# Instance norm over 4 MB units: statistics for pairs of units, and one normalise per engine

## The chip, the cores and the metric

The kernel runs on one core of a Trainium2 chip. The metric is device time in microseconds (us) of one launch, the median of several launches. All data is fp32 and lies in HBM before and after. Launches of one kernel agree within some 0.3%; a difference under 2% counts as "same".

## The reference

```python
# x: (4, 8, 16, 256, 256) fp32, gamma: (8, 16) fp32
mu  = x.mean(axis=(3, 4), keepdims=True)
var = ((x - mu) ** 2).mean(axis=(3, 4), keepdims=True)
out = (x - mu) / np.sqrt(var + 1e-5) * gamma[None, :, :, None, None]
```

There are 512 channels of 65,536 values, 134.22 MB in and 134.22 MB out. Each channel needs its mean and variance before its first value can be written.

## The kernel before

The kernel takes 16 channels at a time, a "unit" of 4 MB: a tile of 128 partitions by 8192 columns, 8 partitions to a channel. There are 32 units and 6 tiles. SyncE issues the loads, ScalarE's sequencer issues the stores. A load into a tile waits until the store out of it has landed. VectorE sums a unit, ScalarE squares it and accumulates, a small matmul adds over the 8 partitions of a channel, and both engines share the normalise.

```python
data = ctx.enter_context(tc.tile_pool(name="data", bufs=6))
...
def load(u):
    t = data.tile([P, F], F32, name="xt")          # P = 128, F = 8192
    for a, b in load_spans.get(u, whole):          # one span: the whole unit
        nc.sync.dma_start(out=t[:, a:b], in_=xv[u, :, a:b])
    tiles[u] = t
for u in range(6):
    load(u)
...
def coefficients(u):
    ...
        nc.vector.reduce_sum(out=sums[:, j : j + 1], in_=t[:, a:b], axis=AX.X)
        for c in range(a, b, SQ):                  # SQ = 4096: two squares
            nc.scalar.activation(
                out=junk[:], in_=t[:, c : c + SQ], func=ACTF.Square,
                accum_out=sqs[:, n : n + 1],
            )
    ... # add the parts up, matmul, copy out of PSUM, negate, variance
    std = stats_pool.tile([P, 1], F32, name="std")
    nc.scalar.activation(out=std[:], in_=var[:], func=ACTF.Sqrt, bias=eps_t[:], scale=1.0)
    ... # reciprocal, scale, shift
for u in range(U):
    scale, shift = coefficients(u)
    t = tiles.pop(u)
    ...
        norm_vector(t, 0, DV, scale, shift)        # DV = 5376 columns
        norm_scalar(t, DV, F, scale, shift)
        nc.scalar.dma_start(out=ov[u], in_=t[:])
    if u + 6 < U:
        load(u + 6)
```

Of the kernel before, what the change touches and what calls it, by code (L numbers as in the profile page):

```python
# [6 lines left out]

F32 = mybir.dt.float32
BF16 = mybir.dt.bfloat16
ALU = mybir.AluOpType  # L10
ACTF = mybir.ActivationFunctionType
AX = mybir.AxisListType


@with_exitstack
def kernel(
    ctx: ExitStack,
    tc: tile.TileContext,
    x: bass.AP,
    gamma: bass.AP,  # L20
    out: bass.AP,
):
    nc = tc.nc
    B, G, C, H, W = x.shape
    P = nc.NUM_PARTITIONS
    HW = H * W
    n_ch = B * G * C
    S = 8
    K = P // S
    F = HW // S  # L30
    U = n_ch // K
    NG = (G * C) // K
    SQ = 4096
    DV = 5376
    assert HW % S == 0 and (G * C) % K == 0 and F % SQ == 0

    xv = x.rearrange("b g c h w -> (b g c h w)").rearrange("(u p f) -> u p f", p=P, f=F)
    ov = out.rearrange("b g c h w -> (b g c h w)").rearrange("(u p f) -> u p f", p=P, f=F)
    gv = gamma.rearrange("g c -> (g c)")

    data = ctx.enter_context(tc.tile_pool(name="data", bufs=6))
    singles = ctx.enter_context(tc.tile_pool(name="singles", bufs=1))
    stats_pool = ctx.enter_context(tc.tile_pool(name="stats", bufs=2))
    psum = ctx.enter_context(tc.tile_pool(name="psum", bufs=2, space=bass.MemoryType.PSUM))
    ctx.enter_context(tc.manual_schedule())

    def spans(widths):
        edges = [0]
        for w in widths:
            edges.append(edges[-1] + w)  # L50
        assert edges[-1] == F
        return list(zip(edges[:-1], edges[1:]))

    load_spans, store_spans = {}, {}
    whole = spans([F])

    tiles = {}

    def load(u):
        t = data.tile([P, F], F32, name="xt")  # L60
        for a, b in load_spans.get(u, whole):
            nc.sync.dma_start(out=t[:, a:b], in_=xv[u, :, a:b])
        tiles[u] = t

    for u in range(6):
        load(u)


    g_row = singles.tile([1, G * C], F32, name="g_row")
    nc.scalar.dma_start(out=g_row[:], in_=gv[None, :])  # L70
    eps_t = singles.tile([P, 1], F32, name="eps_t")
    nc.vector.memset(eps_t[:], 1e-5)
    avg = singles.tile([P, K, S], F32, name="avg")
    nc.gpsimd.memset(avg[:], 1.0 / HW)
    nc.gpsimd.affine_select(
        out=avg[:], in_=avg[:], pattern=[[-S, K], [0, S]], compare_op=ALU.is_ge,
        fill=0.0, base=0, channel_multiplier=1,
    )
    nc.gpsimd.affine_select(
        out=avg[:], in_=avg[:], pattern=[[S, K], [0, S]], compare_op=ALU.is_ge,  # L80
        fill=0.0, base=S - 1, channel_multiplier=-1,
    )
    one = singles.tile([1, 1], F32, name="one")
    nc.vector.memset(one[:], 1.0)
    g_rep = singles.tile([1, NG, K, S], F32, name="g_rep")
    nc.vector.tensor_copy(  # L86
        out=g_rep[:],
        in_=g_row[:].rearrange("o (n k) -> o n k", n=NG).unsqueeze(3).to_broadcast([1, NG, K, S]),
    )
    g_ps = psum.tile([P, NG], F32, name="g_ps", bufs=1)  # L90
    for n in range(NG):
        nc.tensor.matmul(  # L92
            out=g_ps[:, n : n + 1],
            lhsT=g_rep[:, n].rearrange("o k s -> o (k s)"),
            rhs=one[:],
            start=True, stop=True,
        )
    g_col = singles.tile([P, NG], F32, name="g_col")
    nc.vector.tensor_copy(out=g_col[:], in_=g_ps[:])  # L99

    junk = singles.tile([P, SQ], BF16, name="junk")

    def coefficients(u):
        t = tiles[u]
        sums = stats_pool.tile([P, len(load_spans.get(u, whole))], F32, name="sums")
        sqs = stats_pool.tile([P, F // SQ], F32, name="sqs")
        n = 0
        for j, (a, b) in enumerate(load_spans.get(u, whole)):
            nc.vector.reduce_sum(out=sums[:, j : j + 1], in_=t[:, a:b], axis=AX.X)  # L109
            for c in range(a, b, SQ):  # L110
                nc.scalar.activation(  # L111
                    out=junk[:], in_=t[:, c : c + SQ], func=ACTF.Square,
                    accum_out=sqs[:, n : n + 1],
                )
                n += 1
        mv = stats_pool.tile([P, 2], F32, name="mv")
        nc.vector.reduce_sum(out=mv[:, 0:1], in_=sums[:], axis=AX.X)  # L117
        nc.vector.reduce_sum(out=mv[:, 1:2], in_=sqs[:], axis=AX.X)  # L118
        ps = psum.tile([P, 2], F32, name="ps")
        nc.tensor.matmul(  # L120
            out=ps[:], lhsT=avg[:].rearrange("p k s -> p (k s)"), rhs=mv[:],
            start=True, stop=True,
        )
        cm = stats_pool.tile([P, 2], F32, name="cm")
        nc.vector.tensor_copy(out=cm[:], in_=ps[:])  # L125
        nmean = stats_pool.tile([P, 1], F32, name="nmean")
        nc.vector.tensor_scalar(  # L127
            out=nmean[:], in0=cm[:, 0:1], scalar1=-1.0, scalar2=None, op0=ALU.mult,
        )
        var = stats_pool.tile([P, 1], F32, name="var")  # L130
        nc.vector.scalar_tensor_tensor(  # L131
            out=var[:], in0=cm[:, 0:1], scalar=nmean[:], in1=cm[:, 1:2],
            op0=ALU.mult, op1=ALU.add,
        )
        std = stats_pool.tile([P, 1], F32, name="std")
        nc.scalar.activation(out=std[:], in_=var[:], func=ACTF.Sqrt, bias=eps_t[:], scale=1.0)  # L136
        rstd = stats_pool.tile([P, 1], F32, name="rstd")
        nc.vector.reciprocal(out=rstd[:], in_=std[:])  # L138
        scale = stats_pool.tile([P, 1], F32, name="scale")
        g = u % NG  # L140
        nc.vector.tensor_mul(out=scale[:], in0=rstd[:], in1=g_col[:, g : g + 1])  # L141
        shift = stats_pool.tile([P, 1], F32, name="shift")
        nc.vector.tensor_mul(out=shift[:], in0=nmean[:], in1=scale[:])  # L143
        return scale, shift

    def norm_vector(t, a, b, scale, shift):
        nc.vector.tensor_scalar(  # L147
            out=t[:, a:b], in0=t[:, a:b], scalar1=scale[:], scalar2=shift[:],
            op0=ALU.mult, op1=ALU.add,
        )  # L150

    def norm_scalar(t, a, b, scale, shift):
        nc.scalar.activation(  # L153
            out=t[:, a:b], in_=t[:, a:b], func=ACTF.Identity, bias=shift[:], scale=scale[:],
        )

    for u in range(U):
        scale, shift = coefficients(u)
        t = tiles.pop(u)
        if u in store_spans:  # L160
            for j, (a, b) in enumerate(store_spans[u]):
                (norm_scalar if j == 1 else norm_vector)(t, a, b, scale, shift)
            for a, b in store_spans[u]:
                nc.scalar.dma_start(out=ov[u, :, a:b], in_=t[:, a:b])
        else:
            norm_vector(t, 0, DV, scale, shift)
            norm_scalar(t, DV, F, scale, shift)
            nc.scalar.dma_start(out=ov[u], in_=t[:])
        if u + 6 < U:
            load(u + 6)  # L170


# [28 lines left out]
```

## Time and profile before

| | before |
|---|---|
| time, median (lowest to highest) | 628.94 us (628.77 to 628.99), 4 runs |
| span of the profiled execution | 627.1 us |
| VectorE, ScalarE busy | 416.5 us (66%), 336.9 us (54%) |
| data moved | 268.4 MB, 428 GB/s over the span |

From the page of the kernel before: the DMA busy tenths and GB/s of the 40 slices of the span, the two DMA queues (q1 carries the loads, q10 the stores; packets, MB, and the time that their packets took as a share of 16 engines' span), the chain of waits by engine, the group of the VectorE sums (busy us, mean ns | idle before, and what ended it), and the DMA issues (KB each, median us from issue to landing).

```profile
DMA  8999999999999999999999999999999999999997
GB/s 368 435 403 433 435 435 435 433 435 435 435 433 435 435 435 431 433 428 433 435 427 435 431 435 433 433 433 435 435 433 435 435 435 435 433 433 435 435 433 314
...
q1 hardware_dynamic: 4608, 134.22, 49.9%
q10 hardware_dynamic: 4610, 134.22, 49.6%
...
DVE 67%; another core or an unknown queue 23%; PE 3%; DMA 2%; ACT 2%; issue 1%
...
L109 DVE TENSOR_REDUCE sums<-xt 128x1 f32<-128x8192 f32 x32 | 277.9, 8686 | 150.4 <-DMA xt<-in_x_dram 150.4
...
xt<-in_x_dram SPq DMA_DIRECT2D x32, 4096.0 KB, 60.4
out_dram<-xt ACTq DMA_DIRECT2D x32, 4096.0 KB, 41.3
```

The rate sits at 427 to 435 GB/s, mostly 433 to 435, from the fourth slice to the last but one, and the two queues' packets fill 99.5% of the 16 engines' span. The chain names VectorE for 67%, but VectorE itself waits 150 us for loads: it is the DMA engines that bound this kernel. The Trainium skill, "DMA: Bandwidth & Descriptors", section Specifications, gives 435 GB/s as the ceiling of the 16 engines' fabric, and this trace agrees. One slice stands out near the start, the third, with 403. It is the moment at which the first store joins the loads. Seen in windows of 5 us (columns: window, length, busy us of PE, weight loads, VectorE, ScalarE, GpSimd, then clock, DMA busy share, GB/s):

```profile
25.00:30.00 5.00, 0.00 (x0) 0.00 (x0) 5.00 (x2) 4.21 (x2) 0.00 (x0) 1.00 1.00 419
30.00:35.00 5.00, 0.00 (x0) 0.00 (x0) 5.00 (x1) 4.97 (x3) 0.00 (x0) 1.00 0.94 328
35.00:40.00 5.00, 0.59 (x2) 0.50 (x2) 3.75 (x10) 2.12 (x4) 0.00 (x0) 1.00 1.03 446
```

The first store was issued at 27.5 us. Its first data packet moves at 32.5 us. Until then loads go slower: 328 GB/s in one window, with DMA still 94% busy, and single load packets take about 2 us instead of the usual 1.21.

### The profile page before, as it was taken

What the parts mean: (1) busy time and instruction counts of PE and PEld (TensorE: products, weight loads), DVE (VectorE), ACT (ScalarE), POOL (GpSimd) and SP (SyncE); (2) the same over time, 40 slices, a digit from 0 to 9 for tenths busy, and PEclk for the clock granted to TensorE, in tenths of its full rate; (3) what the DMA queues carried; (4) which work ended last, traced back from release to release, by engine and by line L of the source; (5) the groups of instructions that cost most, each with busy time, mean ns of one, the idle gap of its engine ahead of it and who ended that gap; (6) DMA issues with size and microseconds to landing.
All of it is one profiled execution on the core that took longest, in us unless ns stands there. A gap on an engine that the chain in (4) does not pass through costs nothing.

```text
span 627.1 us, 937 instructions
## 1 busy us (share of the span) xinstructions
PE 22.3 (4%) x80; PEld 19.5 (3%) x80; DVE 416.5 (66%) x324; ACT 336.9 (54%) x194; POOL 1.2 (0%) x7
## 2 busy tenths in 40 slices
PE   2000000000000000000000000000000000000000
PEld 2000000000000000000000000000000000000000
DVE  2999657766577665686656866558665577655770
ACT  2877536555456464464634646446554455544560
POOL 0000000000000000000000000000000000000000
DMA  8999999999999999999999999999999999999997
GB/s 368 435 403 433 435 435 435 433 435 435 435 433 435 435 435 431 433 428 433 435 427 435 431 435 433 433 433 435 435 433 435 435 435 435 433 433 435 435 433 314
DMA packets 9224, 268.49 MB, mean 428 GB/s; under 512 B 1025, under 2 KB 1026, under 8 KB 1026
## 3 DMA queue, kind: packets, MB, share of 16 engines
q1 hardware_dynamic: 4608, 134.22, 49.9%
q10 hardware_dynamic: 4610, 134.22, 49.6%
q14 instruction: 6, 0.05, 0.0%
HBM read 134.22 MB, written 134.22 MB: 428 GB/s over the span
## 4 chain that ended last, share of the span: by engine, by line
DVE 67%; another core or an unknown queue 23%; PE 3%; DMA 2%; ACT 2%; issue 1%
DVE sums L109 44%; DVE xt L147 16%; PE ps L120 3%; DMA xt<-in_x_dram 2%; ACT std L136 2%; DVE var L131 1%; DVE rstd L138 1%; DVE cm L125 1%; DVE shift L143 1%; DVE scale L141 1%; DVE nmean L127 1%; DVE mv L117 1%; DVE mv L118 0%
## 5 line engine op out<-in xcount | busy, mean ns | idle before, releaser
L109 DVE TENSOR_REDUCE sums<-xt 128x1 f32<-128x8192 f32 x32 | 277.9, 8686 | 150.4 <-DMA xt<-in_x_dram 150.4
L111 ACT ACTIVATE junk<-xt 128x4096 bf16<-128x4096 f32 x64 | 231.5, 3617 | 166.8 <-DMA xt<-in_x_dram 163.5
L147 DVE TENSOR_SCALAR xt<-xt,scale,shift 128x5376 f32<-128x5376 f32 x32 | 98.5, 3079 | 1.2
L153 ACT ACTIVATE xt<-xt,shift,scale 128x2816 f32<-128x2816 f32 x32 | 87.5, 2734 | 22.0 <-DVE shift L143 22.0
L136 ACT ACTIVATE std<-var,eps_t 128x1 f32<-128x1 f32 x32 | 9.4, 294 | 85.4 <-DVE var L131 85.4
L120 PE MATMUL ps<-mv,avg 128*128 128x2 f32 x64 | 18.7, 362 | 582.9 <-DVE mv L118 582.9
L120 PEld LDWEIGHTS ps<-mv,avg 128*128 128x128 f32 x64 | 16.0, 311 | 585.6 <-DVE mv L118 569.8
L125 DVE COPY cm<-ps 128x2 f32<-128x2 f32 x32 | 5.1, 160 | 21.8 <-PE ps L120 21.8
L138 DVE RECIPROCAL rstd<-std 128x1 f32<-128x1 f32 x32 | 5.2, 164 | 11.6 <-ACT std L136 11.6
L111 ACT ACTIVATION_READ_ACCUMULATOR junk<-xt 128x1 f32 x64 | 11.9, 186 | 0.0
L131 DVE SCALAR_TENSOR_TENSOR var<-cm,nmean 128x1 f32<-128x1 f32 x32 | 7.0, 220 | 1.1
L143 DVE TENSOR_TENSOR shift<-nmean,scale 128x1 f32<-128x1 f32 x32 | 5.1, 159 | 1.1
L141 DVE TENSOR_TENSOR scale<-rstd,g_col 128x1 f32<-128x1 f32 x32 | 5.1, 159 | 1.1
L117 DVE TENSOR_REDUCE mv<-sums 128x1 f32<-128x1 f32 x32 | 4.9, 154 | 1.1
L127 DVE TENSOR_SCALAR nmean<-cm 128x1 f32<-128x1 f32 x32 | 4.9, 153 | 1.1
L118 DVE TENSOR_REDUCE mv<-sqs 128x1 f32<-128x2 f32 x32 | 4.7, 145 | 0.0
L92 PE MATMUL g_ps<-one,g_rep 1*128 1x1 f32 x16 | 3.6, 348 | 2.8 <-DVE g_rep L86 2.8
L92 PEld LDWEIGHTS g_ps<-one,g_rep 1*128 1x128 f32 x16 | 3.5, 325 | 2.8 <-DVE g_rep L86 2.8
L99 DVE COPY g_col<-g_ps 128x8 f32<-128x8 f32 x1 | 0.2, 167 | 3.7 <-PE g_ps L92 3.7
L111 ACT ACT_TABLE_LOAD x1 | 1.3, 1283 | 1.4 <-PEq L185 1.4
L86 DVE COPY g_rep<-g_row 1x1024 f32<-1x1024 f32 x1 | 0.7, 681 | 1.1 <-DMA g_row<-in_gamma_dram 1.1
L136 ACT ACT_TABLE_LOAD x1 | 1.3, 1283 | 0.0
(9 smaller groups left out, 1.5 us busy)
## 6 DMA issues: line engine op xcount, KB each, us to landing
xt<-in_x_dram SPq DMA_DIRECT2D x32, 4096.0 KB, 60.4
out_dram<-xt ACTq DMA_DIRECT2D x32, 4096.0 KB, 41.3
g_row<-in_gamma_dram ACTq DMA_DIRECT2D x1, 0.5 KB
```

Source lines behind the costliest of these rows:

```text
L109: nc.vector.reduce_sum(out=sums[:, j : j + 1], in_=t[:, a:b], axis=AX.X)
L111: nc.scalar.activation(out=junk[:], in_=t[:, c : c + SQ], func=ACTF.Square, accum_out=sqs[:, n : n + 1],)
L117: nc.vector.reduce_sum(out=mv[:, 0:1], in_=sums[:], axis=AX.X)
L120: nc.tensor.matmul(out=ps[:], lhsT=avg[:].rearrange("p k s -> p (k s)"), rhs=mv[:], start=True, stop=True,)
L125: nc.vector.tensor_copy(out=cm[:], in_=ps[:])
L131: nc.vector.scalar_tensor_tensor(out=var[:], in0=cm[:, 0:1], scalar=nmean[:], in1=cm[:, 1:2], op0=ALU.mult, op1=ALU.add,)
L136: nc.scalar.activation(out=std[:], in_=var[:], func=ACTF.Sqrt, bias=eps_t[:], scale=1.0)
L138: nc.vector.reciprocal(out=rstd[:], in_=std[:])
L141: nc.vector.tensor_mul(out=scale[:], in0=rstd[:], in1=g_col[:, g : g + 1])
L143: nc.vector.tensor_mul(out=shift[:], in0=nmean[:], in1=scale[:])
L147: nc.vector.tensor_scalar(out=t[:, a:b], in0=t[:, a:b], scalar1=scale[:], scalar2=shift[:], op0=ALU.mult, op1=ALU.add,)
L153: nc.scalar.activation(out=t[:, a:b], in_=t[:, a:b], func=ACTF.Identity, bias=shift[:], scale=scale[:],)
```

## The change

The intent is to take work off VectorE and ScalarE: one square over 8192 columns instead of two over 4096 (its unused output 8-bit, so that it fits), statistics for two units in one set of small instructions, statistics columns that are written once (no reuse of small tiles), the negated mean straight from the matmul. VectorE then normalises one unit of the pair, ScalarE the other. The last two units are done singly, as before. The diff, cut to its core:

```diff
+    st = singles.tile([P, U, 2], F32, name="st")
+    ...                      # nvar, std, rstd, scale, shift: [P, U] each
-    def coefficients(u):
+    def coefficients(lo, n):
+        hi = lo + n
+        for u in range(lo, hi):
+            t = tiles[u]
+            nc.vector.reduce_sum(out=st[:, u, 0:1], in_=t[:], axis=AX.X)
+            nc.scalar.activation(
+                out=junk[:], in_=t[:], func=ACTF.Square, accum_out=st[:, u, 1:2],
+            )
+        ps = psum.tile([P, n, 2], F32, name="ps")
+        ...                  # one matmul for n units
+        for i in range(n):
+            nc.vector.tensor_scalar(...)       # -variance, straight from PSUM
+        ...                  # square root, reciprocal, scale, shift for n units
...
-    for u in range(U):
-        scale, shift = coefficients(u)
-        ...
+    for u in range(0, U - 2, 2):
+        coefficients(u, 2)
+        norm_vector(u, 0, F)
+        norm_scalar(u + 1, 0, F)
+        for v in (u, u + 1):
+            store(v)
+            if v + AHEAD < U:                  # AHEAD = 6
+                load(v + AHEAD)
+    for u in range(U - 2, U):
+        coefficients(u, 1)
+        norm_vector(u, 0, DV)
+        norm_scalar(u, DV, F)
+        store(u)
```

More of the change, by code (lines that the diff above doesn't have):

```diff
@@ L8 @@
 F32 = mybir.dt.float32
-BF16 = mybir.dt.bfloat16
+U8 = mybir.dt.uint8
 ALU = mybir.AluOpType
@@ L32 @@
     NG = (G * C) // K
-    SQ = 4096
+    AHEAD = 6
     DV = 5376
-    assert HW % S == 0 and (G * C) % K == 0 and F % SQ == 0
+    assert HW % S == 0 and (G * C) % K == 0 and U % 2 == 0 and NG % 2 == 0
     xv = x.rearrange("b g c h w -> (b g c h w)").rearrange("(u p f) -> u p f", p=P, f=F)
@@ L39 @@
     gv = gamma.rearrange("g c -> (g c)")
-    data = ctx.enter_context(tc.tile_pool(name="data", bufs=6))
+    data = ctx.enter_context(tc.tile_pool(name="data", bufs=AHEAD))
     singles = ctx.enter_context(tc.tile_pool(name="singles", bufs=1))
-    stats_pool = ctx.enter_context(tc.tile_pool(name="stats", bufs=2))
-    psum = ctx.enter_context(tc.tile_pool(name="psum", bufs=2, space=bass.MemoryType.PSUM))
+    psum = ctx.enter_context(tc.tile_pool(name="psum", bufs=4, space=bass.MemoryType.PSUM))
     ctx.enter_context(tc.manual_schedule())
-    def spans(widths):
-        edges = [0]
-        for w in widths:
-            edges.append(edges[-1] + w)
-        assert edges[-1] == F
-        return list(zip(edges[:-1], edges[1:]))
-    load_spans, store_spans = {}, {}
-    whole = spans([F])
     tiles = {}
@@ L60, in load @@
         t = data.tile([P, F], F32, name="xt")
-        for a, b in load_spans.get(u, whole):
-            nc.sync.dma_start(out=t[:, a:b], in_=xv[u, :, a:b])
+        nc.sync.dma_start(out=t[:], in_=xv[u])
         tiles[u] = t
-    for u in range(6):
+    for u in range(AHEAD):
         load(u)
@@ L71 @@
     eps_t = singles.tile([P, 1], F32, name="eps_t")
-    nc.vector.memset(eps_t[:], 1e-5)
-    avg = singles.tile([P, K, S], F32, name="avg")
-    nc.gpsimd.memset(avg[:], 1.0 / HW)
+    nc.gpsimd.memset(eps_t[:], 1e-5)
+    one = singles.tile([1, 1], F32, name="one")
+    nc.gpsimd.memset(one[:], 1.0)
+    navg = singles.tile([P, K, S], F32, name="navg")
+    nc.gpsimd.memset(navg[:], -1.0 / HW)
     nc.gpsimd.affine_select(
-        out=avg[:], in_=avg[:], pattern=[[-S, K], [0, S]], compare_op=ALU.is_ge,
+        out=navg[:], in_=navg[:], pattern=[[-S, K], [0, S]], compare_op=ALU.is_ge,
         fill=0.0, base=0, channel_multiplier=1,
@@ L79 @@
     nc.gpsimd.affine_select(
-        out=avg[:], in_=avg[:], pattern=[[S, K], [0, S]], compare_op=ALU.is_ge,
+        out=navg[:], in_=navg[:], pattern=[[S, K], [0, S]], compare_op=ALU.is_ge,
         fill=0.0, base=S - 1, channel_multiplier=-1,
     )
-    one = singles.tile([1, 1], F32, name="one")
-    nc.vector.memset(one[:], 1.0)
+    navg_w = navg[:].rearrange("p k s -> p (k s)")
     g_rep = singles.tile([1, NG, K, S], F32, name="g_rep")
@@ L99 @@
     nc.vector.tensor_copy(out=g_col[:], in_=g_ps[:])
-    junk = singles.tile([P, SQ], BF16, name="junk")
-    def coefficients(u):
-        t = tiles[u]
-        sums = stats_pool.tile([P, len(load_spans.get(u, whole))], F32, name="sums")
-        sqs = stats_pool.tile([P, F // SQ], F32, name="sqs")
-        n = 0
-        for j, (a, b) in enumerate(load_spans.get(u, whole)):
-            nc.vector.reduce_sum(out=sums[:, j : j + 1], in_=t[:, a:b], axis=AX.X)
-            for c in range(a, b, SQ):
-                nc.scalar.activation(
-                    out=junk[:], in_=t[:, c : c + SQ], func=ACTF.Square,
-                    accum_out=sqs[:, n : n + 1],
-                )
-                n += 1
-        mv = stats_pool.tile([P, 2], F32, name="mv")
-        nc.vector.reduce_sum(out=mv[:, 0:1], in_=sums[:], axis=AX.X)
-        nc.vector.reduce_sum(out=mv[:, 1:2], in_=sqs[:], axis=AX.X)
-        ps = psum.tile([P, 2], F32, name="ps")
-        nc.tensor.matmul(
-            out=ps[:], lhsT=avg[:].rearrange("p k s -> p (k s)"), rhs=mv[:],
-            start=True, stop=True,
-        )
-        cm = stats_pool.tile([P, 2], F32, name="cm")
-        nc.vector.tensor_copy(out=cm[:], in_=ps[:])
-        nmean = stats_pool.tile([P, 1], F32, name="nmean")
-        nc.vector.tensor_scalar(
-            out=nmean[:], in0=cm[:, 0:1], scalar1=-1.0, scalar2=None, op0=ALU.mult,
-        )
-        var = stats_pool.tile([P, 1], F32, name="var")
-        nc.vector.scalar_tensor_tensor(
-            out=var[:], in0=cm[:, 0:1], scalar=nmean[:], in1=cm[:, 1:2],
-            op0=ALU.mult, op1=ALU.add,
-        )
-        std = stats_pool.tile([P, 1], F32, name="std")
-        nc.scalar.activation(out=std[:], in_=var[:], func=ACTF.Sqrt, bias=eps_t[:], scale=1.0)
-        rstd = stats_pool.tile([P, 1], F32, name="rstd")
-        nc.vector.reciprocal(out=rstd[:], in_=std[:])
-        scale = stats_pool.tile([P, 1], F32, name="scale")
-        g = u % NG
-        nc.vector.tensor_mul(out=scale[:], in0=rstd[:], in1=g_col[:, g : g + 1])
-        shift = stats_pool.tile([P, 1], F32, name="shift")
-        nc.vector.tensor_mul(out=shift[:], in0=nmean[:], in1=scale[:])
-        return scale, shift
@@ L146, in norm_vector @@
-    def norm_vector(t, a, b, scale, shift):
-        nc.vector.tensor_scalar(
-            out=t[:, a:b], in0=t[:, a:b], scalar1=scale[:], scalar2=shift[:],
-            op0=ALU.mult, op1=ALU.add,
-        )
-    def norm_scalar(t, a, b, scale, shift):
-        nc.scalar.activation(
-            out=t[:, a:b], in_=t[:, a:b], func=ACTF.Identity, bias=shift[:], scale=scale[:],
-        )
-    for u in range(U):
-        scale, shift = coefficients(u)
-        t = tiles.pop(u)
-        if u in store_spans:
-            for j, (a, b) in enumerate(store_spans[u]):
-                (norm_scalar if j == 1 else norm_vector)(t, a, b, scale, shift)
-            for a, b in store_spans[u]:
-                nc.scalar.dma_start(out=ov[u, :, a:b], in_=t[:, a:b])
-        else:
-            norm_vector(t, 0, DV, scale, shift)
-            norm_scalar(t, DV, F, scale, shift)
-            nc.scalar.dma_start(out=ov[u], in_=t[:])
-        if u + 6 < U:
-            load(u + 6)
+    junk = singles.tile([P, F], U8, name="junk")
@@ new lines @@
+    st = singles.tile([P, U, 2], F32, name="st")
+    nvar = singles.tile([P, U], F32, name="nvar")
+    std = singles.tile([P, U], F32, name="std")
+    rstd = singles.tile([P, U], F32, name="rstd")
+    scale = singles.tile([P, U], F32, name="scale")
+    shift = singles.tile([P, U], F32, name="shift")
+    def coefficients(lo, n):
[7 more added lines that the diff above has]
+        ps = psum.tile([P, n, 2], F32, name="ps")
+        nc.tensor.matmul(
+            out=ps[:].rearrange("p n c -> p (n c)"), lhsT=navg_w,
+            rhs=st[:, lo:hi].rearrange("p n c -> p (n c)"), start=True, stop=True,
+        )
+        for i in range(n):
+            nc.vector.tensor_scalar(
+                out=nvar[:, lo + i : lo + i + 1], in0=ps[:, i, 0:1], scalar1=ps[:, i, 0:1],
+                scalar2=ps[:, i, 1:2], op0=ALU.mult, op1=ALU.add,
+            )
+        nc.scalar.activation(
+            out=std[:, lo:hi], in_=nvar[:, lo:hi], func=ACTF.Sqrt, bias=eps_t[:], scale=-1.0,
+        )
+        nc.vector.reciprocal(out=rstd[:, lo:hi], in_=std[:, lo:hi])
+        g = lo % NG
+        nc.vector.tensor_mul(out=scale[:, lo:hi], in0=rstd[:, lo:hi], in1=g_col[:, g : g + n])
+        nc.vector.tensor_mul(out=shift[:, lo:hi], in0=ps[:, :, 0], in1=scale[:, lo:hi])
@@ new lines, in norm_vector, with norm_scalar, store @@
+    def norm_vector(u, a, b):
+        t = tiles[u]
+        nc.vector.tensor_scalar(
+            out=t[:, a:b], in0=t[:, a:b], scalar1=scale[:, u : u + 1],
+            scalar2=shift[:, u : u + 1], op0=ALU.mult, op1=ALU.add,
+        )
+    def norm_scalar(u, a, b):
+        t = tiles[u]
+        nc.scalar.activation(
+            out=t[:, a:b], in_=t[:, a:b], func=ACTF.Identity,
+            bias=shift[:, u : u + 1], scale=scale[:, u : u + 1],
+        )
+    def store(u):
+        nc.scalar.dma_start(out=ov[u], in_=tiles.pop(u)[:])
```

## The prediction

> **What bounds the kernel now: the DMA engines.** The page's queue part counts 134.22 MB loaded and 134.22 MB stored; the 40-slice table reads 433 to 435 GB/s in most slices. 268.4 MB at 435 GB/s take 617 us of the 627.1 us span. This agrees with the Trainium skill, "DMA: Bandwidth & Descriptors", Specifications, which puts the fabric ceiling at 435 GB/s. VectorE is busy 66%, ScalarE 54%; by the table of waits they sit idle 150 and 164 us for loads. The chain of waits gives 67% to VectorE, but each unit's link ends with about 5.1 us in which VectorE waits for data (timeline), so shorter VectorE work only lengthens that wait: the unit period is 19.35 us, and 8.39 MB at 435 GB/s take 19.3 us.
>
> The other 10 us are fixed: about 2 us until data flows, 1 us of slow first packets, 1.3 us lost when stores first join the loads (windows, 30 to 35 us: 328 GB/s), some 3 us because the 16 engines end at different times, 1.4 us to the end.
>
> **What the change removes, adds, moves.** Per unit go: the overhead of one of two squares (a 4096-wide one is 3.62 us plus 0.19; an 8192-wide one, estimated from these, 7.0 plus 0.19), two small VectorE reductions (0.15 us each), the PSUM copy (0.16), the negation (0.15), and half of the square root, reciprocal, multiplies and matmul. VectorE normalises one whole unit, estimated 4.6 us from 3.08 us for 5376 columns; ScalarE the other, estimated 7.2 us from 2.73 us for 2816. Busy per pair: VectorE 2x8.7+4.6+1 = 23 us, ScalarE 2x7.2+7.2+0.3 = 22 us, against 38.7 us of DMA. Neither becomes the limit, and none of the savings is on the limiting resource.
>
> What moves is when buffers come free. From the landing of a pair's later load to the issue of its stores take about 8.7+2.2+7.2 = 18 us (before: about 14 us for a unit). First stores go out at about 41 us instead of 27.5; six loads alone keep DMA full until 60 us. In the steady state stores then run about 4 units behind loads instead of 3; when a pair's stores are issued, about one 4 MB store (some 18 us of shared bandwidth) is still queued, and a load too. So DMA should stay full. The last store should be issued near 600 us (now 612.8) but queue behind others; before, the slowest engine was still busy with the previous store then (it landed at 616.5), so almost nothing is gained. Fewer instructions mean less instruction fetch on the DMA engines: below 1 us.
>
> **Prediction:** 628.2 us, range 626.3 to 630.5. Faster by over 2%: 0.02; within 2%: 0.96; slower by over 2%: 0.02.
>
> **What would show it.** Right: slices still at 433 to 435 GB/s; VectorE busy falls to about 370 us, ScalarE goes to about 350 us, their waits for loads grow; stores first issued near 41 us, the last near 600; pair period 38.7 us. Wrong: mid-run slices well below 430 GB/s, or load issues that come after the load queue has emptied, once per pair.
>
> **What would make it wrong.** If the late, paired freeing of buffers drains a queue and one queue alone doesn't fill the bandwidth (in the trace loads alone run at 433 GB/s, stores alone too); if ScalarE's 8-bit output is so much slower than bf16 that a pair takes over 38 us; if the dip at the stores' start grows or repeats.

## The result and the profile after

The changed kernel takes 643.04 us (642.08 to 644.26, 4 runs), the kernel before 628.94 us. The ratio is 1.0226 (95% interval 1.0207 to 1.0245), slower. A ratio here is the mean time of one kernel's fast runs over that of the other's of the same rounds, so not quite the ratio of the medians.

From the page of the changed kernel, the same parts as above:

```profile
DMA  9999999999999999999999999999999999999994
GB/s 377 437 394 451 422 414 420 424 428 418 426 417 422 422 430 430 415 432 416 430 430 414 430 412 430 432 412 437 418 424 424 428 428 408 434 420 424 437 431 208
...
q1 hardware_dynamic: 4608, 134.22, 50.3%
q10 hardware_dynamic: 4610, 134.22, 48.4%
...
DMA 68%; DVE 12%; another core or an unknown queue 12%; ACT 2%; PE 1%; issue 0%; SPq 0%; ACTq 0%
...
L103 DVE TENSOR_REDUCE st<-xt 128x1 f32<-128x8192 f32 x32 | 277.8, 8685 | 217.8 <-DMA xt<-in_x_dram 217.8
...
xt<-in_x_dram SPq DMA_DIRECT2D x32, 4096.0 KB, 36.8
out_dram<-xt ACTq DMA_DIRECT2D x32, 4096.0 KB, 47.7
```

VectorE fell to 369.0 us busy and ScalarE rose to 349.2, as intended; VectorE's sums now wait 217.8 us for loads instead of 150.4. So compute did not become the limit. The DMA engines are busy all the time and yet move mostly 412 to 437 GB/s, with a mean of 418 over the span where the kernel before has 428.

The queue lines say where. Before, loads took 49.9% of 627.1 us, which is 312.9 us, and stores 49.6%, 311.0 us. After, loads took 50.3% of 642.6 us, 323.2 us, and stores 48.4%, 311.0 us. The same 4608 load packets cost 10.3 us more on each engine; the stores cost nothing more. The middle of the run in one window, 100 to 560 us, kernel before:

```profile
100.00:560.00 460.00, 14.08 (x48) 12.01 (x48) 305.47 (x241) 244.31 (x143) 0.00 (x0) 1.00 1.00 433
```

and the changed kernel:

```profile
100.00:560.00 460.00, 6.16 (x22) 5.51 (x22) 260.44 (x89) 246.43 (x68) 0.00 (x0) 1.00 1.00 424
```

The DMA busy share is 1.00 in both, at 433 and at 424 GB/s. The share counts the whole time of a packet, also when it takes 1.46 us instead of 1.21 (below). So it can't show this loss; the rate does.

Finer windows of the changed kernel show that the loss is not spread evenly:

```profile
97.00:102.00 5.00, 0.00 (x0) 0.00 (x0) 1.05 (x1) 3.14 (x2) 0.00 (x0) 1.00 0.99 426
102.00:107.00 5.00, 0.00 (x0) 0.00 (x0) 5.00 (x1) 5.00 (x1) 0.00 (x0) 1.00 1.01 400
...
137.00:142.00 5.00, 0.00 (x0) 0.00 (x0) 0.98 (x1) 3.09 (x2) 0.00 (x0) 1.00 1.04 446
142.00:147.00 5.00, 0.00 (x0) 0.00 (x0) 5.00 (x1) 5.00 (x1) 0.00 (x0) 1.00 0.95 360
147.00:152.00 5.00, 0.00 (x0) 0.00 (x0) 2.70 (x1) 1.14 (x2) 0.00 (x0) 1.00 1.00 433
```

The dips come at the moments when one store DMA ends and the next begins, which I call a hand-over of the stores. The landing of a store can be read from the time at which SyncE issues the load that waited for it, and the landing of a load from the time at which VectorE starts to sum it. From the timeline of the changed kernel (VectorE's row, then SyncE's):

```profile
100.95 8.69 DVE L103 TENSOR_REDUCE st<-xt 128x1 f32<-128x8192 f32 x1 [4.59 <-DMA xt<-in_x_dram]
...
104.96 0.33 SPq L50 DMA_DIRECT2D xt<-in_x_dram  x1
```

Here a load ends at 100.9 us and a store ends 4.0 us later. The same from the timeline of the kernel before:

```profile
207.01 0.33 SPq L62 DMA_DIRECT2D xt<-in_x_dram  x1
...
209.39 8.69 DVE L109 TENSOR_REDUCE sums<-xt 128x1 f32<-128x8192 f32 x1 [5.09 <-DMA xt<-in_x_dram]
```

Here the store ends first, at 207.0 us, and a load 2.4 us later. Loads and stores share the bandwidth in equal parts, so each takes about 19.4 us per unit, and the offset between their hand-overs repeats from unit to unit: in the kernel before it is 16.9 us from the first store to the 29th.

The trace holds every packet (32 KB, one partition's row) and the 16 completion records of each DMA, one per DMA engine. I use three figures from them. The *offset* is the time from the last landing of a load to the landing of a store, each taken at the first of its 16 engines. The *excess* is how much longer packets took than the median packet's 1.213 us, added up and divided by 16, so per engine; for one hand-over of the stores, over the packets from midway to the hand-over before to midway to the next. The *spread* is the time between the first and the last engine's landing of one DMA. A packet does not name its engine, but packets of one engine follow each other to the hundredth of a us, so a sequence can be put together. One engine of the kernel before, and one of the changed kernel, at a store's hand-over (L load, S store, start in us, duration in brackets; packets of 4 bytes left out):

```
before  S203.18(1.21) L204.39(1.21) L205.61(1.21) S206.82(1.21) S208.03(1.21)
after   S101.63(1.21) L102.84(1.46) L104.31(1.48) S105.78(1.21) L106.99(1.21)
```

Loads and stores take turns packet by packet. That agrees with the Trainium skill, "DMA: Bandwidth & Descriptors", section Queues, rings and completion order, which says that each engine goes round-robin between its queues, a packet at a time; in this trace a packet is one 32 KB row. At a hand-over the turn of the store queue goes to a 4-byte packet of 0.01 us, with which each DMA ends on each engine, so two loads follow each other. In the kernel before that costs nothing. In the changed kernel the two loads take 0.52 us longer together. Of the changed kernel's excess between 60 and 560 us, over nine tenths lies within four packets before and after such a turn.

Summed over the run, the packets' excess is 12.9 us per engine (loads 12.5) against 2.0 us before. That is 10.9 of the 15.5 us by which the spans differ. The rest is the slowest engine losing more than the mean one: the last store landed 11.0 us later than before in the mean of the engines and 15.5 us later on the slowest, and its landings spread over 10.4 us instead of 2.4.

### The profile page after: what moved, and what is told of

The parts are those of the page before. It is cut to its first block, busy times and chain, and to the rows that moved or that the text cites. A ratio compares the mean times of both kernels' runs of the same rounds, so it can differ in the third digit from the quotient of the medians.

```text
span 642.6 us, 570 instructions
## 1 busy us (share of the span) xinstructions
PE 13.1 (2%) x50; PEld 12.0 (2%) x50; DVE 369.0 (57%) x134; ACT 349.2 (54%) x100; POOL 1.3 (0%) x9
## 3 DMA queue, kind: packets, MB, share of 16 engines
q1 hardware_dynamic: 4608, 134.22, 50.3%
q10 hardware_dynamic: 4610, 134.22, 48.4%
## 4 chain that ended last, share of the span: by engine, by line
DMA 68%; DVE 12%; another core or an unknown queue 12%; ACT 2%; PE 1%; issue 0%; SPq 0%; ACTq 0%
DMA out_dram<-xt 36%; DMA xt<-in_x_dram 32%; DVE st L103 8%; DVE xt L127 3%; ACT xt L134 1%; PE ps L108 1%; DVE nvar L113 0%; SPq L50 0%; ACT std L117 0%; ACT L117 0%; DVE rstd L120 0%; DVE scale L122 0%; DVE shift L123 0%; ACTq L134 0%
## 5 line engine op out<-in xcount | busy, mean ns | idle before, releaser
L103 DVE TENSOR_REDUCE st<-xt 128x1 f32<-128x8192 f32 x32 | 277.8, 8685 | 217.8 <-DMA xt<-in_x_dram 217.8
L104 ACT ACTIVATE junk<-xt 128x8192 uint8<-128x8192 f32 x32 | 225.0, 7030 | 207.7 <-DMA xt<-in_x_dram 206.8
L134 ACT ACTIVATE xt<-xt,shift,scale 128x8192 f32<-128x8192 f32 (+1 forms) x17 | 113.7, 6688 | 11.6 <-DVE shift L123 11.6
L127 DVE TENSOR_SCALAR xt<-xt,scale,shift 128x8192 f32<-128x8192 f32 (+1 forms) x17 | 74.4, 4374 | 0.9 <-DVE shift L123 0.3
L117 ACT ACTIVATE std<-nvar,eps_t 128x2 f32<-128x2 f32 (+1 forms) x17 | 5.0, 296 | 42.5 <-DVE nvar L113 42.5
L108 PE MATMUL ps<-st,navg 128*128 128x4 f32 (+1 forms) x34 | 9.5, 351 | 594.6 <-DVE st L103 569.8
L108 PEld LDWEIGHTS ps<-st,navg 128*128 128x128 f32 x34 | 8.5, 312 | 595.6 <-issue 570.7
L113 DVE TENSOR_SCALAR nvar<-ps 128x1 f32<-128x1 f32 x32 | 7.8, 283 | 12.9 <-PE ps L108 12.9
L120 DVE RECIPROCAL rstd<-std 128x2 f32<-128x2 f32 (+1 forms) x17 | 2.8, 166 | 7.5 <-ACT std L117 7.5
L104 ACT ACTIVATION_READ_ACCUMULATOR junk<-xt 128x1 f32 x32 | 6.0, 186 | 0.0
## 6 DMA issues: line engine op xcount, KB each, us to landing
xt<-in_x_dram SPq DMA_DIRECT2D x32, 4096.0 KB, 36.8
out_dram<-xt ACTq DMA_DIRECT2D x32, 4096.0 KB, 47.7
```

What stands on the lines that cost most here:

```text
L103: nc.vector.reduce_sum(out=st[:, u, 0:1], in_=t[:], axis=AX.X)
L104: nc.scalar.activation(out=junk[:], in_=t[:], func=ACTF.Square, accum_out=st[:, u, 1:2],)
L108: nc.tensor.matmul(out=ps[:].rearrange("p n c -> p (n c)"), lhsT=navg_w, rhs=st[:, lo:hi].rearrange("p n c -> p (n c)"), start=True, stop= ...
L113: nc.vector.tensor_scalar(out=nvar[:, lo + i : lo + i + 1], in0=ps[:, i, 0:1], scalar1=ps[:, i, 0:1], scalar2=ps[:, i, 1:2], op0=ALU.mult, ...
L117: nc.scalar.activation(out=std[:, lo:hi], in_=nvar[:, lo:hi], func=ACTF.Sqrt, bias=eps_t[:], scale=-1.0,)
L120: nc.vector.reciprocal(out=rstd[:, lo:hi], in_=std[:, lo:hi])
```

## Experiments

The theories:

- **A**: what costs is a store's hand-over that comes shortly after a load's hand-over. The first store's time sets the offset.
- **B**: the load queue is too shallow at that moment (issue to landing fell from 60.4 to 36.8 us).
- **C**: too many stores stand in the store queue (41.3 to 47.7 us).
- **D**: any delay of the first store costs. **E**: VectorE's and ScalarE's work in SBUF stretches the loads.

### Everything but the pairs

```diff
-    for u in range(0, U - 2, 2):
-        coefficients(u, 2)
-        ...
+    for u in range(U):
+        coefficients(u, 1)
+        norm_vector(u, 0, DV)
+        norm_scalar(u, DV, F)
+        store(u)
+        if u + AHEAD < U:
+            load(u + AHEAD)
```

> All parts of the change (once-used statistics columns, one 8192-wide square, 8-bit output of the squares, fused variance) except the pairing: one unit at a time, the normalise split over both engines as in the kernel before. If the loss comes from the pairing, by whatever mechanism, this runs as the kernel before: 627 to 630 us, load issue to landing near 60 us, store near 41 us, no stretched load packets after the first store. If the loss comes from one of the other parts, it stays near 643 us.

It took 628.11 us (627.88 to 628.33), ratio to the kernel before 0.9988 (0.9973 to 1.0003), loads 59.5 and stores 42.7 us from issue to landing, no excess. So the wide square, its 8-bit output and the once-used columns cost nothing; the loss comes with the pairs.

### Four buffers

```diff
-    data = ctx.enter_context(tc.tile_pool(name="data", bufs=6))
+    data = ctx.enter_context(tc.tile_pool(name="data", bufs=4))
-    for u in range(6):
+    for u in range(4):
...
-        if u + 6 < U:
-            load(u + 6)
+        if u + 4 < U:
+            load(u + 4)
```

> The kernel before with 4 data buffers instead of 6: stores queue as deep as before (issue to landing near 41 us), but only about one load stands in the load queue when a store ends, as in the changed kernel or fewer. Theory B (the load queue is too shallow at the moment a store hands over to the next) expects 640 us or more, with slices at 415 to 430 GB/s. Theory A (the moment of hand-over of the stores against that of the loads) and theory C (three or four stores waiting in the store queue) expect 627 to 632 us, as long as the load queue is never empty; if it does run empty, DMA share falls visibly and the run tells nothing between them.

It took 630.52 us (628.98 to 636.89), ratio 1.0055 (0.9997 to 1.0113). Loads landed 27.6 us after issue, a shallower queue than in the changed kernel; stores 35.4 us (near 41 expected). In the profiled run there was no excess. The offset was 17.1 us at the first store and 10.6 us from the third on: no load packet moved from 53 to 57 us, while the next load waited for the first store, so here it was not the first store's time alone that set the offset. The run speaks against B; one of its four timed runs was some 1% slower, and why is not known.

### The first store 2.3 us later, nothing else

```diff
+        if u == 0:
+            idle = singles.tile([P, 1], F32, name="idle")
+            nc.scalar.activation(
+                out=junk[:], in_=t[:, :SQ], func=ACTF.Square, accum_out=idle[:],
+            )
         std = stats_pool.tile([P, 1], F32, name="std")
```

> The kernel before with one extra 3.8 us ScalarE square in unit 0 only, so that all stores start about 3.8 us later: depths of both queues as before, but stores now hand over about 1 to 4 us after the loads do, instead of some 2.4 us before them. Theory A expects a loss of the changed kernel's kind and size, about 0.4 us per unit, so 638 to 645 us, with stretched load packets at each store's end. Theories B and C expect 628 to 630 us: the delay is hidden behind six queued loads.

It took 669.42 us (668.14 to 670.88), ratio 1.0645 (1.0626 to 1.0665). This is the kernel before with one useless 3.8 us instruction at the very start; it does the same work in the same order, and it lost 40 us. The first store went out at 29.8 us (27.5 before; part of the 3.8 us fell into ScalarE's idle time), and the offset became 2.4 us. Its GB/s line and two windows, to 500 us and from there:

```profile
GB/s 376 437 409 435 428 407 431 428 419 429 419 427 419 415 431 427 411 431 411 431 414 431 419 417 429 427 423 423 419 423 431 425 427 431 304 416 272 204 233 259
```

```profile
100.00:500.00 400.00, 11.14 (x38) 9.51 (x38) 247.16 (x191) 198.72 (x116) 0.00 (x0) 1.00 1.00 423
500.00:669.00 169.00, 4.69 (x16) 4.00 (x16) 100.25 (x80) 79.86 (x46) 0.00 (x0) 1.00 0.81 341
```

Up to 500 us it runs at 423 GB/s like the changed kernel. The direction and the kind of loss are what A expected; the size is not (638 to 645 us expected). Slower packets make up only 13.1 us per engine of the 42 us by which the span grew, little more than in the changed kernel (10.9); over a third of it is in store packets. The other 29 us are time in which engines moved nothing. The excess falls unevenly on the engines: the spread of one load's landings grew to 47 us, more than two units. A load waits for the slowest engine's store, so at the end the fast engines have nothing queued and stand idle, DMA share 0.81.

### The changed kernel with its first store at a load's hand-over

```diff
+        if lo == 0:
+            idle = singles.tile([P, 2], F32, name="idle")
+            for j, w in enumerate((F, 2304)):
+                nc.scalar.activation(
+                    out=junk[:, :w], in_=tiles[0][:, :w], func=ACTF.Square,
+                    accum_out=idle[:, j : j + 1],
+                )
         nc.scalar.activation(
             out=std[:, lo:hi], ...
```

> The changed kernel with about 9.6 us of extra ScalarE squares in the first pair only, so that the first store starts some 6.5 us later, at the moment when one load hands over to the next (about 51 us), as it does in the kernel before. Depths of the queues hardly change. Theory A expects that the loss goes: 627 to 632 us. Theories B and C expect about 643 us, unchanged.

It took 627.45 us (627.12 to 627.72), ratio 0.9977 (0.9962 to 0.9992). Useless work of 9.6 us made the changed kernel 15.6 us faster. The offset came to 12.1 us rather than to that of the kernel before (it had been 14.5 us at the first store; then no load packet moved from 73 to 76 us), and there was no excess. Loads stood even less deep (24.7 us) and stores deeper (56.6 us) than in the changed kernel, which rules out B and C as the cause.

### Where the lossy range lies

Four more kernels move the first store of the kernel before, by dummy squares of other widths in unit 0:

```diff
+            for j, w in enumerate(widths):   # (3264,), (4096, 1088), (4096, 2816) or (4096, 4096, 1856)
+                nc.scalar.activation(
+                    out=junk[:, :w], in_=t[:, :w], func=ACTF.Square,
+                    accum_out=idle[:, j : j + 1],
+                )
```

The first, with the one width 3264:

> The kernel before with about 3.1 us of extra ScalarE work in unit 0 only, so that the first store is issued about 1.6 us later (near 29.1 us; 27.5 before, 28.4 in the run of single units that lost nothing, 29.8 in the late-store run that lost 40 us). Theory A says that the loss comes when a store hands over shortly after a load does (+1.8 to +3.6 us in the two lossy runs; none at -2.4, -1.1 or at +10.5 and +12 us). This one should land close to 0 us and finds the window's lower edge: between 628 us and 670 us; no loss would put the edge above about 0, a loss below it.

With 4096 and 2816:

> The kernel before with the first store issued about 5 us later (near 32.5 us), so that stores should hand over some 5 us after loads. Theory A: finds the window's upper edge; if the window is a few us wide as the lossy runs suggest, little or no loss, under 634 us. A theory by which any delay of the first store costs time (rival D: the later the stores start, the worse) expects more than the 669 us of the run with 2.3 us of delay.

With 4096, 4096 and 1856:

> The kernel before with the first store issued about 8 us later (near 35.5 us), stores handing over some 8 us after loads, nearer to the middle of a load. Theory A: no loss, 627 to 631 us. Rival D: a larger loss than at 2.3 us of delay, over 669 us.

With 4096 and 1088, run later:

> The kernel before with the first store issued about 3.6 us later (near 31.1 us). The steps so far: issue at 29.0 us gave hand-over of stores 0.2 us after loads and no loss, 29.8 gave 2.4 us and a loss of 40 us, 32.4 gave 7.2 us and no loss. This should land at about 4.8 us. It bounds the lossy range: about 628 us if the range ends below 4.8 us, over 635 us if it reaches there.

They took 629.58, 628.68, 628.66 and 631.61 us, one timed run each (state unknown), at offsets of 0.2, 7.2, 13.3 and 4.8 us. At 4.8 us there was hardly any excess; the landings spread over 4.9 us. D falls: later starts lost nothing. All kernels with whole-unit loads, in the order of the offset (excess of loads and stores per hand-over and engine, mean over the 24 hand-overs of the third to the 26th store in the profiled run):

| kernel | first store issued, us | offset, us | excess, us | time, us |
|---|---|---|---|---|
| before, 1.6 us later | 29.0 | 0.2 | 0.02 | 629.58 |
| before, 2.3 us later | 29.8 | 2.4 to 2.5 until midway | 0.45 | 669.42 |
| copy without computing | 29.4 | 2.5 | 0.36 | 641.66 |
| **changed kernel** | 39.8 | 2.4 to 3.5 | 0.41 | 643.04 |
| before, 3.6 us later | 30.8 | 4.8 | 0.03 | 631.61 |
| copy, later | 32.2 | 7.2 | 0.00 | 627.07 |
| before, 5 us later | 32.4 | 7.2 | 0.01 | 628.68 |
| changed, first pair on ScalarE | 42.4 | 8.3 | 0.00 | 627.21 |
| before, four buffers | 27.7 | 10.6 | 0.01 | 630.52 |
| changed, 9.6 us of dummy work | 46.2 | 12.1 | 0.00 | 627.45 |
| before, 8 us later | 35.5 | 13.3 | 0.01 | 628.66 |
| **before** | 27.5 | 16.9 | 0.01 | 628.94 |
| everything but the pairs | 28.4 | 18.2 | 0.01 | 628.11 |

The offset repeats every 19.4 us, so 18.2 is also 1.1 us ahead of a load's hand-over. The loss stands in a narrow range, above 0.2 and below 4.8 us, and at none of the other offsets tried. Per hand-over the three lossy kernels lose about the same; the kernel of 669 us loses more time because its engines drift apart.

### Loads split in two

```diff
-        for a, b in load_spans.get(u, whole):
-            nc.sync.dma_start(out=t[:, a:b], in_=xv[u, :, a:b])
+        for a, b in ((0, P),) if u < 6 else ((0, 96), (96, P)):
+            nc.sync.dma_start(out=t[a:b], in_=xv[u, a:b])
```

> The kernel before, but from the seventh load on each 4 MB load is issued as two DMAs, of 96 and of 32 partitions (same packets of 32 KB, same bytes, same order): now a load DMA ends at three quarters of each unit, about 2.5 us ahead of each store's end, where the kernel before has none. Nothing else moves. If it is the hand-over from one load DMA to the next shortly ahead of a store's that costs (theory A), this loses time as the late-store run did: 640 us or more, with stretched load packets. If what counts is where in the unit, in time or address, the store ends, it runs like the kernel before, 628 to 630 us. If the extra DMAs hold back issues (more completion semaphores in use), the issue times show it and the run tells less.

It took 749.28 us, but it settles nothing about hand-overs. "Nothing else moves" was wrong: between 100 and 600 us it ran at 360 GB/s, and the load packets were slow throughout (median 1.53 us instead of 1.213 after 100 us), not at hand-overs alone:

```profile
100.00:600.00 500.00, 12.33 (x42) 10.52 (x42) 266.27 (x210) 213.21 (x124) 0.00 (x0) 1.00 1.00 360
```

The Trainium skill, "SBUF — State Buffer", section Door 1: The DMA port swizzle, gives a possible reason: a block of 32 partitions reaches only 8 of the 16 ports by which DMA enters SBUF. No run here tests that, or separates it from the effect looked for. Loads also came to wait for other loads' completion semaphores. Whether it is the end of a load DMA as such that matters, or something else that comes once per unit, stays open.

### A copy

All computing is taken out; the output is wrong (it is the input). Two versions differ in one dummy square of unit 0, and so in the first store's time:

```diff
-        scale, shift = coefficients(u)
-        ...
+        if u == 0:
+            for j, w in enumerate(widths):   # (4096,) * 4 + (1088,), or (4096,) * 5
+                nc.scalar.activation(
+                    out=junk[:, :w], in_=t[:, :w], func=ACTF.Square,
+                    accum_out=idle[:, j : j + 1],
+                )
+        nc.scalar.activation(out=t[:, 0:8], in_=t[:, 0:8], func=ACTF.Identity)
+        nc.scalar.dma_start(out=ov[u], in_=t[:])
```

> A copy, wrong on purpose: loads and stores of the kernel before without sums, squares, statistics and normalise; only an 8-column instruction of ScalarE stands between a unit's load and its store, and dummy squares in unit 0 let the first store go out near 30 us, as in the late-store run. Theory A, the DMA engines alone: stores hand over about 2.4 us after loads and the loss is there without any computing, 640 us or more. Rival E (the stretched loads come from VectorE and ScalarE working in SBUF at that moment): no loss, 626 to 630 us.

> The same copy with one more dummy square in unit 0, the first store going out near 32.5 us, as in the run that lost nothing at 7.2 us between hand-overs. Theory A: 626 to 630 us. If the copy loses here too, what the other copy loses says nothing about the hand-overs.

They took 641.66 and 627.07 us (one timed run each, state unknown). The GB/s line of the first copy:

```profile
GB/s 377 434 401 426 399 428 430 426 426 426 424 432 428 424 422 428 428 422 428 422 424 430 424 424 422 418 438 414 424 426 418 426 426 426 430 424 424 428 434 266
```

and of the second:

```profile
GB/s 369 436 403 436 436 436 434 436 436 436 436 424 428 434 428 436 436 434 436 437 434 436 436 421 428 430 436 436 434 436 436 436 434 436 430 421 432 432 436 369
```

A copy with a 2.5 us offset loses as much as the changed kernel, with VectorE and ScalarE all but idle after the first unit. E falls: the loss needs no computing. It is shared out otherwise than in the changed kernel, though: between 60 and 560 us 5.9 of the 10.0 us of excess per engine lie in store packets, where the changed kernel has 0.4 of 10.6.

### A version without waste

```diff
-        norm_vector(u, 0, F)
+        (norm_scalar if u == 0 else norm_vector)(u, 0, F)
         norm_scalar(u + 1, 0, F)
```

> The changed kernel with one thing altered: in the first pair ScalarE normalises both units, one after the other, so that the first store goes out near 42.6 us instead of 39.8 and no work is added. Theory A: stores should then hand over some 5 to 7 us after loads, outside the lossy range if that ends below 5 us: 627 to 629 us, a version with nothing wasted that beats both kernels by a little. If the loss comes from pairing itself, or the range reaches to 6 us, it stays over 638 us.

It took 627.21 us (626.99 to 627.40), ratio to the kernel before 0.9974 (0.9957 to 0.9991). It is the changed kernel with one instruction moved to the other engine, once; the offset is 8.3 us. Its queues and issues:

```profile
q1 hardware_dynamic: 4608, 134.22, 49.9%
q10 hardware_dynamic: 4610, 134.22, 49.7%
...
xt<-in_x_dram SPq DMA_DIRECT2D x32, 4096.0 KB, 30.0
out_dram<-xt ACTq DMA_DIRECT2D x32, 4096.0 KB, 51.5
```

The loads' packets are back to 49.9% of a 625.6 us span, 312.2 us (323.2 in the changed kernel), with the load queue shallower still than there. This is the change as it was meant, and its worth is about 1.6 us, which counts as "same". Part of it may come from fewer instructions (570 instead of 937, and 3 instead of 6 DMA packets of the instruction queue), as the last store's landings spread over 1.3 instead of 2.4 us; that is argued, not shown.

## Why the prediction was wrong

- *The bound.* Right: the DMA engines bound both kernels. Their rate was taken to stay at 435 GB/s, see below.
- *The costs of instructions.* Right: the wide square 7.03 us (7.0 estimated), the whole normalise 4.55 us on VectorE (4.6) and 7.22 us on ScalarE (7.2), VectorE 369.0 us busy (370), ScalarE 349.2 (350), waits for loads up.
- *The first store.* Issued at 39.8 us (41 predicted). Right in time, and wrong in its meaning. That "six loads alone keep DMA full until 60 us" is not what failed (DMA stood at 9 tenths in every slice but the last), but the first store's time also fixes the offset between the hand-overs of both queues for the rest of the run. The change moved it from 16.9 to about 3 us, into the lossy range.
- *"So DMA should stay full."* This is the step that failed. The queues never ran empty in the steady state (each load was issued at least 6 us before the one ahead of it landed), the busy share stayed at 1.00, and the rate still fell from 433 to 424 GB/s, as load packets were stretched at nearly every hand-over of the stores. "Not empty" was taken for "at full rate". The period of a pair came to 40.0 us (stores of the third pair issued at 96.4 us, of the fifteenth at 576.85, twelve periods) instead of 38.7, and the last store went out at 615.5 us instead of 600.
- *What would make it wrong.* "If the dip at the stores' start grows or repeats" was named, and in this form it is what happened: stretched load packets return at the hand-overs. All ways to lose over 2% together got a share of 0.02, and this one was not costed. The dip in the profile before was a sign that load packets can be slowed when the store queue does something. Whether both dips have one cause is not shown: the kernels that lose nothing have the first one too.

What is shown: the loss comes and goes with the first store's time, in the kernel before, in the changed kernel and in a copy; it stands in packets around the stores' hand-overs, in the changed kernel nearly all in load packets; queue depth, the compute engines and the other parts of the change are not the cause. What is open: why a store's hand-over 2 to 4 us after a load's makes the engine wait, when one at 0.2 us or at 7 us does not, why it hits some of the 16 engines so much harder, and why it falls on loads in one kernel and on stores as well in another.

## What to carry to other kernels

In this kernel, bound by a load stream and a store stream of equal, large DMAs, the time of the first store fixed how the two streams interleave for the rest of the run, as long as both streams kept moving, and so a harmless change in the first unit moved the whole by 2 to 6%. Expect that it can happen in kernels of this form. When a change leaves DMA at 9 tenths busy but the GB/s line falls, compare the two queues' shares of packet time, then the times at which loads and stores land against each other. Before judging such a change, run it at two or three start times of the first store; the change here lost 2.3% or won 0.3% by that alone.

## What the Trainium skill lacked or had wrong

- "DMA: Bandwidth & Descriptors", Queues, rings and completion order: it describes the round-robin between queues but no cost that depends on when one queue changes to its next DMA against the other. Here a store's hand-over 2.4 to 3.5 us after a load's cost 0.36 to 0.45 us per engine each time, 13 to 40 us in a run of 629 us; at the other offsets tried it cost 0.03 us or less.
- The same page: no word that a store joining running loads slows them. Here the rate fell to 328 GB/s over 5 us, and the first store's packets came some 5 us after its issue.
- "DMA: Bandwidth & Descriptors", Specifications and Bandwidth: one sentence of Bandwidth says that for transfers between HBM and SBUF the HBM side, about 358 GB/s per core, binds. It lacks the condition, which the same section gives further up, that both cores of an HBM domain stream. This kernel, on one core, moved 433 to 435 GB/s for most of its span, loads and stores together (what the neighbouring core did is not on record), so the 435 of the fabric is the figure that held.
